# Empty space between x and the weights, four reorderings, in a two-model forward pass on one core

## The chip, the cores and the metric

The kernel runs on one core of a Trainium2 chip. The metric is device time in microseconds. Before the change the median of three runs is 2032.73 us (2032.72 to 2033.11). The one execution that the profiler recorded took 2020.3 us, of which its span, from the first to the last instruction, is 2018.6 us.

## The reference

One sequence of 256 tokens, width 1024, float32, goes through two models, one after the other.

- The first: a norm, `h @ w_in`, a gated linear recurrence over heads of 64 (`S_t = diag(f_t) S_{t-1} + k_t v_t^T`, `o_t = S_t^T q_t`), a short causal convolution, a gated merge and `w_out`; then a layer of 16,384 single-neuron experts. A query `h @ w_query` is scored against two sets of 128 keys per head, the best 16 of each set make 256 candidates, the best 16 of these are kept, and `out = sum gate * gelu(u_i . h) * v_i` over them.
- The second: two layers, each `x + 0.5 * swiglu(norm(x))`, a mixer (stick-breaking attention with pooling in the even layer, block attention in the odd one), and again `x + 0.5 * swiglu(norm(x))` with 2816 hidden units.
- A norm stands at the end of each.

## The kernel before, in words

Every activation is held transposed, 128 channels by 256 tokens. `x`, `xh` and `xl` are tiles of 8 x 256 float32 for the residual and the two halves of the normed input. Every weight matrix is cut into blocks of 128 x 128, 5220 in all, and eight blocks in the order of use are a chunk, one transfer of 512 KB.

A product at nearly full float32 precision takes three matmuls in the type float32r (`mm3`, lines 149 to 154): the weights' high half times the input's high half, the weights' high half times the input's low half, the weights' low half times the input's high half. The weights are the stationary operand, 128 x 128; the input is the moving one, 128 x 256. For this ScalarE rounds a raw chunk into `whi` (line 80) and VectorE subtracts to get `wlo` (line 87). There are five buffers for `raw`, four for `whi`, three for `wlo`, each 4096 bytes in a partition.

`boundary(c)` (line 91) runs when the program comes to a new chunk. It queues the splits and loads of the chunks ahead, then functions that were hooked to a chunk number (`hook`, line 124), then one step of each running generator (`side`, line 127). So the order of each engine's queue is the order of the Python code. All loads go through SyncE's queue.

Places that the change touches:

- **Start** (lines 412 to 454). `x` comes in pieces of two rows and the first three chunks in halves, by turns; `vec` (all gains and small vectors, 108 columns) and `ident` go through ScalarE's queue. Then pairs of rows are scaled into `xh` and `xl` and the half chunks are split.
- **Recurrence** (`hgrn`, line 677). The generator `decays` (line 695) makes cumulative decays at six block lengths. At each: two Exp on ScalarE (lines 713, 714), an addition into `su` (line 717) that may only overwrite `su` when the second Exp has read it, then a `yield`, then an addition into `pr` (line 720), which the next length's Exp reads. The main generator multiplies the results into `qk` (lines 763, 764) and TensorE makes scores of them (line 742).
- **Rank table** (line 863). Three chunks into the query stage a hook loads all keys, 1 MB; one chunk later another loads `iota`, and VectorE at once makes `ranks` from it.
- **ffn** (line 487). 22 blocks of 128 hidden units: gate and up products from `xh`, `xl`; the activation is split into `ah`, `al` (tiles of 1024 bytes); then the down products, eight blocks of weights for each `ah`. The four calls are a0, b0, a1, b1.
- **Last norm** (`final`, line 369). Six small matmuls sum the squares, POOL and VectorE make `1/sqrt`, TensorE spreads it over the partitions, VectorE copies it to `R`, and `x` is multiplied by it in four pieces (VectorE three, POOL one of two rows) that are stored as they come.

Where the operands lie follows from the order and sizes of the tiles. In the built program `xh` and `xl` begin at bytes 9,344 and 17,536 of each partition, the weights' buffers at 53,056 and every 4,096 on. Taken modulo 512 that is 128 for the inputs and 320 for the weights. A block is 512 bytes and a row of the input 1024, so the distance from the weights to the moving operand, modulo 512, is the same for every block: 320 for `xh`, `xl`; 0 for `ah`, `al` in all four ffn stages and for `oh`, `ol` in the odd mixer; 384 for `oh`, `ol`, `mph`, `mpl` in the even mixer; 160 for `mh`, `ml`, `yah`, `ybh` of the first mixer.

Of the kernel before, what the change touches and what calls it, by code (L numbers as in the profile page):

```python
# [10 lines left out]
F32 = mybir.dt.float32  # L11
# [21 lines left out]
STAGES = 3  # L33
RANK = 256
PACE = 1.0
FF = 22
NBLOCKS = 5220
NCHUNK = -(-NBLOCKS // CB)
# [11 lines left out]
class Net:  # L50
# [318 lines left out]
    def final(self):  # L369
        nc = self.nc  # L370
        V, S, G, mm = nc.vector, nc.scalar, nc.gpsimd, nc.tensor.matmul
        ps = self.sm.tile([P, 512], F32, name="sm")
        parts = [self.ssum] + self.last
        for t in range(2):
            for j, q in enumerate(parts):
                mm(ps[:, t:t + 1], q[:, t * P:(t + 1) * P], self.ones, start=(t == 0 and j == 0),
                   stop=(j == len(parts) - 1), skip_group_check=True)
        r = self.rsqrt_b(*self.rsqrt_a(ps[:, 0:2], 2, 1.0 / D))
        ps = self.sm.tile([P, 2, T], F32, name="sm")
        self.bcast(ps[:, 0, :], r)  # L380
        R = self.sqp.tile([P, T], F32, name="R", bufs=1)
        V.tensor_copy(R, ps[:, 0, :])
        for i in range(4):
            s = slice(2 * i, 2 * i + 2)
            if i < 3:
                V.tensor_tensor(self.x[:, s, :], self.x[:, s, :],
                                R[:, None, :].to_broadcast([P, 2, T]), op=ALU.mult)
            else:
                for k in (6, 7):
                    G.tensor_tensor(self.x[:, k, :], self.x[:, k, :], R, op=ALU.mult)  # L390
            o = self.out[2 * i * P:(2 * i + 2) * P, :].rearrange("(k p) t -> p k t", p=P)
            (nc.sync if i < 3 else nc.scalar).dma_start(o, self.x[:, s, :])

    def out_tail(self, name, ks, sl, first, alpha, gcol):
        for i in range(KD // 2):
# [6 lines left out]
    def run(self, first=0, last=99):  # L402
        nc, tc = self.nc, self.tc
        pool = tc.tile_pool
        with pool(name="base", bufs=1) as base, pool(name="sqp", bufs=2) as self.sqp, \
                pool(name="small", bufs=2) as self.small, \
                pool(name="rawp", bufs=self.NRAW) as self.rawp, \
                pool(name="hip", bufs=self.NHI) as self.hip, \
                pool(name="lop", bufs=self.NLO) as self.lop, \
                pool(name="accp", bufs=4, space=PSUM) as self.acc, \  # L410
                pool(name="smp", bufs=4, space=PSUM) as self.sm:
            A = self.A
            self.x = base.tile([P, KD, T], F32, name="x")
            self.xh = base.tile([P, KD, T], F32R, name="xh")
            self.xl = base.tile([P, KD, T], F32R, name="xl")
            self.vec = base.tile([P, NV], F32, name="vec")
            self.ident = base.tile([P, P], F32, name="ident")
            self.ones = base.tile([P, 1], F32, name="ones")
            self.mhalf = base.tile([P, 16], F32, name="mhalf")
            nc.scalar.dma_start(self.vec, A["vec"])  # L420
            nc.scalar.preload_act_table_set("natural_log_exp_and_others")
            hw = CB * P // 2
            for i in range(self.NRAW):
                if i > 2:
                    self.load_chunk(i)
                    continue
                self.raws[i] = self.rawp.tile([P, CB * P], F32, name="raw")
                for j in range(2):
                    if i < 2:
                        k = slice(4 * i + 2 * j, 4 * i + 2 * j + 2)  # L430
                        nc.sync.dma_start(self.x[:, k, :], A["x"][:, k, :])
                    h = slice(j * hw, j * hw + hw)
                    nc.sync.dma_start(self.raws[i][:, h], A["w"][i][:, h])
            nc.scalar.dma_start(self.ident, A["ident"])
# [6 lines left out]
            for i in range(self.NHI):  # L441
                if i > 2:
                    self.split_hi(i)
                    continue
                self.his[i] = self.hip.tile([P, CB * P], F32R, name="whi")
                self.los[i] = self.lop.tile([P, CB * P], F32R, name="wlo")
                for j in range(2):
                    if i < 2:
                        for k in (4 * i + 2 * j, 4 * i + 2 * j + 1):
                            self.norm_k(k, self.gain(GAINS[first]))  # L450
                    h = slice(j * hw, j * hw + hw)
                    nc.scalar.copy(self.his[i][:, h], self.raws[i][:, h])  # L452
                    nc.vector.tensor_tensor(self.los[i][:, h], self.raws[i][:, h], self.his[i][:, h],
                                            op=ALU.subtract)
# [13 lines left out]
            for i, st in enumerate(stages):  # L468
                if i > last:
                    break  # L470
                if i < first:
                    continue
                nxt = None if i == len(stages) - 1 else self.gain(GAINS[i + 1])
                st(nxt)
            if last < 90:
                for _ in self.norm_steps():
                    pass
                self.drain_sides()
                for k in range(KD):
# [7 lines left out]
    def ffn(self, tag, gcol):  # L487
        nc = self.nc
        with self.tc.tile_pool(name="ffn" + tag, bufs=3) as wp, \
                self.tc.tile_pool(name="ffa" + tag, bufs=8) as ap:  # L490
            ah = {}

            def ev(f, ps):
                gu = wp.tile([P, 2, T], F32, name="gu")
# [40 lines left out]
    def mixer1(self, gcol):  # L535
        nc = self.nc
        V, S = nc.vector, nc.scalar
        with self.tc.tile_pool(name="m1", bufs=1) as p1, self.tc.tile_pool(name="m1t", bufs=2) as tp:
# [17 lines left out]
            for z in (u[:, :, 0:2], su, ends[:, :, 1], sa, sb):  # L556
                nc.gpsimd.memset(z, 0.0)

            def vt(n):
                return tp.tile([P, 2, T], F32, name=n)  # L560
# [116 lines left out]
    def hgrn(self, ph, qp, E, pr, su, sa, sb, kk, qq, v, masks, oT, hg, late, outs):  # L677
# [7 lines left out]
        def half(t, c, which):  # L685
            return flat(t).rearrange("p (n two c) -> p n two c", two=2, c=c)[:, :, which, :]
# [8 lines left out]
        def decays():  # L695
# [15 lines left out]
            for li, c in enumerate(levels):  # L711
                up, low, nb = half(pr, c, 1), half(pr, c, 0), cols // (2 * c)
                S.activation(half(E[:, li], c, 1), up, AF.Exp)
                S.activation(half(E[:, li], c, 0), half(su, c, 0), AF.Exp)
                if li == nl - 1:
                    return
                V.tensor_tensor(half(su, c, 0), half(su, c, 0),
                                up[:, :, c - 1:c].to_broadcast([P, nb, c]), op=ALU.add)
                yield
                V.tensor_tensor(up, up, low[:, :, c - 1:c].to_broadcast([P, nb, c]), op=ALU.add)  # L720
        self.side(decays())
        yield
# [117 lines left out]
    def peer(self, gcol):  # L840
        nc = self.nc
        V, S, mm = nc.vector, nc.scalar, nc.tensor.matmul
        with self.tc.tile_pool(name="pe", bufs=1) as p1, self.tc.tile_pool(name="peh", bufs=2) as hp:
# [14 lines left out]
            live = top[0]  # L858
            kr, qr, xr = rows(8), rows(6), rows(8)
            keys = flat[:, kr * T:(kr + 8) * T].rearrange("p (h s n) -> p h s n", h=PH, s=2)  # L860
            self.hook(self.c + 3, lambda: nc.sync.dma_start(keys, self.A["keys"]))

            def consts():
                nc.sync.dma_start(self.iota, self.A["iota"])
                V.tensor_scalar(self.ranks, self.iota[:, 0:TOPK], float(RANK), None, op0=ALU.mult)
            self.hook(self.c + 4, consts)
            qv = [acts[:, qr + 2 * i:qr + 2 * i + 2, :] for i in range(3)]
            xn = acts[:, xr:xr + 8, :]

# [562 lines left out]
```

## Time and profile before

| | |
|---|---|
| median of three runs | 2032.73 us |
| the profiled execution, its own time | 2020.3 us |
| its span | 2018.6 us |
| TensorE busy | 1984.7 us, 98% |
| VectorE, ScalarE, POOL busy | 66%, 53%, 8% |
| mean granted clock of TensorE | 0.994 |
| data moved | 349.5 MB, 173 GB/s |

TensorE is the engine to look at. Its matmuls overlap, each shown for some 0.28 us though the next starts after about 0.118 us, so that its busy share says only where it stood still, not how fast it went; the pace is read from starts, or from how many matmuls fall into a window.

### The profile page before, as it was taken

The page shows a single profiled execution, that of the slowest core. Times are in us where ns is not written, and L with a number is a line of the kernel's source. Part 1 is how long each engine was busy: PE and PEld are TensorE (multiplying, and loading weights), DVE is VectorE, ACT ScalarE, POOL GpSimd, SP SyncE. Part 2 cuts the span into 40 slices and gives each one's busy share as a digit, 9 for nine tenths or more (in the row PEclk, how much of TensorE's full clock was granted, in tenths as well). Part 3 has the DMA queues.
Part 4 walks back from the last instruction along what each step waited for, and adds up shares of the span by engine and source line. Part 5 has one row for each costly group of instructions (what it writes and reads, how often), then busy time and mean ns, then how long its engine had stood idle before and what let it go on. Part 6 is the DMA issues. An engine that isn't in the chain of part 4 may idle for free.

```text
span 2018.6 us, 40539 instructions
## 1 busy us (share of the span) xinstructions
PE 1984.7 (98%) x16678; PEld 1956.7 (97%) x16678; DVE 1340.0 (66%) x2122; ACT 1072.6 (53%) x1754; POOL 170.2 (8%) x159
## 2 busy tenths in 40 slices
PE   8899899999999999999999999999999999999998
PEld 8899899999999999999999999999999999899997
DVE  6867578877777655555567556665566556666555
ACT  6454444557776545445464445654455445555444
POOL 2000244100000000000000001110001001231001
PEclk9999999999999999999999999999999999999999
DMA  7335445544444566666555555455555555435553
GB/s 243 128 130 182 164 168 189 188 167 141 143 139 134 164 194 196 193 195 197 191 167 193 184 188 192 146 172 185 187 180 187 188 186 179 160 129 188 185 184 103
DMA packets 97465, 349.50 MB, mean 173 GB/s; under 512 B 10880, under 2 KB 12416, under 8 KB 97152
## 3 DMA queue, kind: packets, MB, share of 16 engines
q1 hardware_dynamic: 96720, 346.53, 51.8%
q8 instruction: 130, 2.13, 0.4%
q10 hardware_dynamic: 560, 0.38, 0.1%
q14 instruction: 55, 0.45, 0.1%
HBM read 345.82 MB, written 1.05 MB: 172 GB/s over the span
## 4 chain that ended last, share of the span: by engine, by line
PE 96%; DVE 2%; DMA 1%; ACT 1%; issue 0%; POOL 0%; DVEq 0%; SPq 0%; ACTq 0%
PE acc L152 22%; PE acc L153 21%; PE acc L154 21%; PE sm L152 8%; PE sm L154 8%; PE sm L153 7%; PE sm L1127 3%; PE acc L176 1%; PE acc L177 1%; PE acc L178 1%; DVE wlo L87 1%; PE sm L742 0%; DMA iota<-in_iota 0%; PE sm L889 0%; POOL rs L251 0%
## 5 line engine op out<-in xcount | busy, mean ns | idle before, releaser
L87 DVE TENSOR_TENSOR wlo<-raw,whi 128x1024 fp32r<-128x1024 f32 x629 | 769.9, 1226 | 437.8 <-issue 241.7
L80 ACT CAST whi<-raw 128x1024 fp32r<-128x1024 f32 x650 | 679.2, 1049 | 499.1 <-PE acc L153 288.3
L152 PE MATMUL acc<-xh,whi 128*128 128x256 f32 x2848 | 804.9, 283 | 8.1 <-ACT whi L452 7.2
L154 PE MATMUL acc<-xh,wlo 128*128 128x256 f32 x2848 | 794.5, 279 | 3.7 <-DVE wlo L87 3.7
L153 PE MATMUL acc<-xl,whi 128*128 128x256 f32 x2848 | 794.5, 279 | 0.3
L152 PEld LDWEIGHTS acc<-xh,whi 128*128 128x128 f32 x2848 | 537.1, 189 | 13.2 <-ACT whi L452 7.2
L154 PEld LDWEIGHTS acc<-xh,wlo 128*128 128x128 f32 x2848 | 536.7, 188 | 4.7 <-DVE wlo L87 4.5
L153 PEld LDWEIGHTS acc<-xl,whi 128*128 128x128 f32 x2848 | 536.9, 189 | 0.9 <-DVE xl L220 0.7
L152 PE MATMUL sm<-xh,whi 128*128 128x256 f32 x1280 | 359.1, 281 | 0.0
L153 PE MATMUL sm<-xl,whi 128*128 128x256 f32 x1280 | 357.2, 279 | 0.0
L154 PE MATMUL sm<-xh,wlo 128*128 128x256 f32 x1280 | 357.1, 279 | 0.0
L152 PEld LDWEIGHTS sm<-xh,whi 128*128 128x128 f32 x1280 | 240.6, 188 | 0.0
L154 PEld LDWEIGHTS sm<-xh,wlo 128*128 128x128 f32 x1280 | 240.5, 188 | 0.0
L153 PEld LDWEIGHTS sm<-xl,whi 128*128 128x128 f32 x1280 | 239.9, 187 | 0.0
L154 PE MATMUL acc<-ah,wlo 128*128 128x256 f32 x704 | 199.5, 283 | 0.0
L152 PE MATMUL acc<-ah,whi 128*128 128x256 f32 x704 | 199.3, 283 | 0.0
L153 PE MATMUL acc<-al,whi 128*128 128x256 f32 x704 | 199.2, 283 | 0.0
L152 PEld LDWEIGHTS acc<-ah,whi 128*128 128x128 f32 x704 | 134.9, 192 | 0.0
L154 PEld LDWEIGHTS acc<-ah,wlo 128*128 128x128 f32 x704 | 134.6, 191 | 0.0
L153 PEld LDWEIGHTS acc<-al,whi 128*128 128x128 f32 x704 | 134.6, 191 | 0.0
L239 POOL TENSOR_TENSOR ssum<-ssum,sq 128x256 f32<-128x256 f32 x54 | 61.0, 1130 | 797.4 <-issue 575.6
L497 ACT ACTIVATE s<-gu 128x256 f32<-128x256 f32 x88 | 36.7, 418 | 119.8 <-DVE gu L314 119.5
(318 smaller groups left out, 1942.9 us busy)
## 6 DMA issues: line engine op xcount, KB each, us to landing
raw<-in_w SPq DMA_DIRECT2D x650, 512.0 KB, 3.7
raw<-in_w SPq DMA_DIRECT2D x6, 256.0 KB, 5.6
x<-in_x SPq DMA_DIRECT2D x4, 256.0 KB, 5.0
acts<-in_keys SPq DMA_DIRECT2D x1, 1024.0 KB, 7.7
out_dram<-x SPq DMA_DIRECT2D x3, 256.0 KB, 2.2
inv<-in_inv SPq DMA_DIRECT2D x1, 512.0 KB, 6.1
E<-in_masks SPq DMA_DIRECT2D x1, 320.0 KB, 7.9
out_dram<-x ACTq DMA_DIRECT2D x1, 256.0 KB, 2.4
```

The lines of the kernel that those rows point to most:

```text
L80: self.nc.scalar.copy(self.his[i], self.raws[i])
L87: e.tensor_tensor(self.los[i], self.raws[i], self.his[i], op=ALU.subtract)
L152: mm(out, wh, xh, start=start, stop=False, skip_group_check=True)
L153: mm(out, wh, xl, start=False, stop=False, skip_group_check=True)
L154: mm(out, wl, xh, start=False, stop=stop, skip_group_check=True)
L176: mm(pss[t], xh, wh, start=(k == 0), stop=False)
L177: mm(pss[t], xh, wl, start=False, stop=False)
L178: mm(pss[t], xl, wh, start=False, stop=(k == KD - 1))
L239: nc.gpsimd.tensor_tensor(self.ssum, self.ssum, sq, op=ALU.add)
L497: nc.scalar.activation(s, gu[:, 0, :], AF.Silu)
L1127: nc.tensor.matmul(ps[:, q, :], a[:, q, :], b[:, q, :], start=True, stop=True, skip_group_check=True)
```

## The change

Five edits, of which the first is one of place and the others are of order.

- **Empty space.** An unused tile of 128 bytes now lies between `xl` and all that follows, the weights' buffers among it. Another lies ahead of `ah` in each ffn stage: 64, 128, 256 and 384 bytes in a0, b0, a1, b1. The distance modulo 512 from the weights to the moving operand becomes 192 for `xh`, `xl` (from 320) and 64, 128, 256 and 384 for `ah`, `al` (from 0). The other tiles move along with the weights and keep theirs.
- **Rank table.** The keys come in eight pieces, one a chunk, `iota` with the first, and `ranks` is made 12 chunks later than before.
- **Recurrence.** The `yield` in `decays` stands ahead of the addition into `su` rather than behind it.
- **First loads.** The first gain alone, then the first chunk in quarters through ScalarE's queue, `x` in single rows through SyncE's; the rest later. VectorE instead of POOL clears `sa`.
- **Last norm.** The sums go part by part; VectorE and ScalarE read the spread factor from two PSUM tiles, VectorE without a copy; POOL multiplies one row and VectorE seven.

```diff
+SKEW = {"x": 128, "a0": 64, "b0": 128, "a1": 256, "b1": 384}
...
-        for t in range(2):
-            for j, q in enumerate(parts):
+        for j, q in enumerate(parts):
+            for t in range(2):
...
-        V.tensor_copy(R, ps[:, 0, :])
...
+        S.copy(R, ps[1][:, 0, :])
+        G.tensor_tensor(self.x[:, 7, :], self.x[:, 7, :], R, op=ALU.mult)
+        rows = lambda a, b: self.out[a * P:b * P, :].rearrange("(k p) t -> p k t", p=P)
+        for a, b, q in ((0, 2, nc.sync), (2, 4, nc.sync), (4, 6, nc.sync), (6, 7, nc.sync), (7, 8, nc.scalar)):
+            if b < 8:
+                V.tensor_tensor(self.x[:, a:b, :], self.x[:, a:b, :],
+                                ps[0][:, 0:1, :].to_broadcast([P, b - a, T]), op=ALU.mult)
+            q.dma_start(rows(a, b), self.x[:, a:b, :])
...
             self.xl = base.tile([P, KD, T], F32R, name="xl")
+            base.tile([P, SKEW["x"] // 4], F32, name="skew")
...
+            nc.scalar.dma_start(self.vec[:, g0:g0 + KD], A["vec"][:, g0:g0 + KD])
...
+            for k in range(4):
+                nc.scalar.dma_start(self.raws[0][:, two[k]], A["w"][0][:, two[k]])
+                nc.sync.dma_start(self.x[:, k, :], A["x"][:, k, :])
...
             ah = {}
+            ap.tile([P, SKEW[tag] // 4], F32, name="skew", bufs=1)
...
+                yield
                 V.tensor_tensor(half(su, c, 0), half(su, c, 0),
                                 up[:, :, c - 1:c].to_broadcast([P, nb, c]), op=ALU.add)
-                yield
...
-            self.hook(self.c + 3, lambda: nc.sync.dma_start(keys, self.A["keys"]))
-
-            def consts():
-                nc.sync.dma_start(self.iota, self.A["iota"])
-                V.tensor_scalar(self.ranks, self.iota[:, 0:TOPK], float(RANK), None, op0=ALU.mult)
-            self.hook(self.c + 4, consts)
+            for h in range(PH):
+                self.hook(self.c + 2 + h, lambda h=h: nc.sync.dma_start(keys[:, h], self.A["keys"][:, h]))
+
+            self.hook(self.c + 2, lambda: nc.sync.dma_start(self.iota, self.A["iota"]))
+            self.hook(self.c + 16, lambda: V.tensor_scalar(self.ranks, self.iota[:, 0:TOPK], float(RANK), None,
+                                                           op0=ALU.mult))
```

The order of TensorE's matmuls stays as it was, but for the six small ones of the last norm. Two places on VectorE move.

VectorE's queue in the recurrence before, from the first block length on; `su` and `pr` are the running sums, `t` and `u` belong to the convolution:

```order
L751 TENSOR_TENSOR qk<-E,kk 128x1024
L717 TENSOR_TENSOR su<-su,pr 128x128x4
L314 TENSOR_TENSOR t<-acc,R 128x512
L587 TENSOR_TENSOR u<-t 128x256
L87 TENSOR_TENSOR wlo<-raw,whi 128x1024
L720 TENSOR_TENSOR pr<-pr 128x128x4
L717 TENSOR_TENSOR su<-su,pr 128x64x8
L87 TENSOR_TENSOR wlo<-raw,whi 128x1024
```

The same place now, with the new line numbers (729 is the addition into `su`, 731 that into `pr`, 89 the split):

```order
L762 TENSOR_TENSOR qk<-E,kk 128x1024
L316 TENSOR_TENSOR t<-acc,R 128x512
L598 TENSOR_TENSOR u<-t 128x256
L89 TENSOR_TENSOR wlo<-raw,whi 128x1024
L729 TENSOR_TENSOR su<-su,pr 128x128x4
L731 TENSOR_TENSOR pr<-pr 128x128x4
L89 TENSOR_TENSOR wlo<-raw,whi 128x1024
L729 TENSOR_TENSOR su<-su,pr 128x64x8
```

Each addition into `su` moved behind the next chunk's split, next to the addition into `pr`.

VectorE's queue at the start of the query before; `rs` are the small tiles of the norm's `1/sqrt`:

```order
L87 TENSOR_TENSOR wlo<-raw,whi 128x1024 x4
L865 TENSOR_SCALAR ranks<-iota 128x16
L246 TENSOR_SCALAR rs<-sm 128x2
L87 TENSOR_TENSOR wlo<-raw,whi 128x1024
L256 TENSOR_TENSOR rs<-rs 128x2
```

And now:

```order
L89 TENSOR_TENSOR wlo<-raw,whi 128x1024 x4
L248 TENSOR_SCALAR rs<-sm 128x2
L89 TENSOR_TENSOR wlo<-raw,whi 128x1024
L258 TENSOR_TENSOR rs<-rs 128x2
L259 TENSOR_TENSOR rs<-rs 128x2
```

`ranks` left this place; it now stands 48 rows further on, amid the search for the best keys.

## Rows read from the trace of the kernel before

**Rows 1.** The page: busy time, share of the span, instructions of each engine.

```profile
PE 1984.7 (98%) x16678; PEld 1956.7 (97%) x16678; DVE 1340.0 (66%) x2122; ACT 1072.6 (53%) x1754; POOL 170.2 (8%) x159
```

**Rows 2.** Waits of TensorE, whole span: us in total, times, longest.

```profile
PE sm L291 <- DVE rs L259: 9.3, 2, 7.4
PE acc L152 <- ACT whi L452: 7.2, 1, 7.2
PE sm L742 <- DVE qk L764: 4.4, 1, 4.4
```

**Rows 3.** Groups by line, TensorE: names, shapes xcount | busy us, mean ns | idle before.

```profile
L152 PE MATMUL acc<-xh,whi 128*128 128x256 f32 x2848 | 804.9, 283 | 8.1 <-ACT whi L452 7.2 <-ACT xh L219 0.9
...
L152 PE MATMUL sm<-xh,whi 128*128 128x256 f32 x1280 | 359.1, 281 | 0.0
...
L152 PE MATMUL acc<-ah,whi 128*128 128x256 f32 x704 | 199.3, 283 | 0.0
```

**Rows 4.** Windows: PE, PEld, DVE, ACT, POOL busy (instructions), clock, DMA share, GB/s.

```profile
300.00:400.00 100.00, 100.00 (x852) 100.00 (x851) 88.15 (x307) 48.65 (x57) 29.15 (x12) 1.00 0.55 187
720.00:1020.00 300.00, 300.00 (x2650) 300.00 (x2649) 172.15 (x221) 149.41 (x220) 0.00 (x0) 1.00 0.60 194
```

**Rows 5.** Timeline of TensorE, first and last of a pass: start us, us, instruction.

```profile
190.13 0.28 PE L154 MATMUL acc<-mh,wlo 128*128 128x256 f32 x1
...
212.31 0.28 PE L154 MATMUL acc<-mh,wlo 128*128 128x256 f32 x1
...
1226.33 0.29 PE L152 MATMUL acc<-ah,whi 128*128 128x256 f32 x1
...
1240.38 0.28 PE L152 MATMUL acc<-ah,whi 128*128 128x256 f32 x1
...
1314.71 0.28 PE L154 MATMUL acc<-oh,wlo 128*128 128x256 f32 x1
...
1325.75 0.28 PE L154 MATMUL acc<-oh,wlo 128*128 128x256 f32 x1
```

**Rows 6.** Waits of TensorE from 60 to 90 us (the recurrence).

```profile
PE acc L154 <- DVE wlo L87: 2.6, 2, 1.9
```

**Rows 7.** Waits of VectorE from 60 to 82 us.

```profile
DVE su L717 <- ACT E L714: 4.9, 4, 1.2
```

**Rows 8.** Windows with the clock at half, columns as in rows 4.

```profile
82.70:87.60 4.90, 4.89 (x30) 4.78 (x31) 4.49 (x6) 3.04 (x4) 0.00 (x0) 0.50 0.59 203
235.10:237.80 2.70, 2.70 (x14) 2.70 (x13) 2.67 (x5) 0.00 (x0) 0.00 (x0) 0.50 0.66 228
```

**Rows 9.** Waits of VectorE from 210 to 250 us (start of the query).

```profile
DVE ranks L865 <- DMA iota<-in_iota: 8.5, 1, 8.5
```

**Rows 10.** Timeline of SyncE's queue there: start, us, issues.

```profile
222.81 0.38 SPq L861 DMA_DIRECT2D acts<-in_keys  x1
...
223.90 1.05 SPq L864 DMA_DIRECT2D iota<-in_iota  x1
```

**Rows 11.** Timeline of ScalarE from 0 us: first work after the loads.

```profile
5.68 0.91 ACT L219 ACTIVATE xh<-x,vec 128x256 fp32r<-128x256 f32 x2 [3.17 <-DMA vec<-in_vec]
6.50 0.60 ACT L452 CAST whi<-raw 128x512 fp32r<-128x512 f32 x1
```

**Rows 12.** Timeline of TensorE from 0 us.

```profile
7.15 0.58 PE L152 MATMUL acc<-xh,whi 128*128 128x256 f32 x1 [7.15 <-ACT whi L452]
```

**Rows 13.** Timeline of TensorE at the end.

```profile
2007.98 0.38 PE L376 MATMUL sm<-ones,R 128*128 128x1 f32 x2
...
2008.67 0.36 PE L376 MATMUL sm<-ones,R 128*128 128x1 f32 x2
```

**Rows 14.** Timeline of VectorE at the end.

```profile
2011.72 0.42 DVE L382 COPY R<-sm 128x256 f32<-128x256 f32 x1 [0.92 <-PE sm L291]
2012.18 2.95 DVE L386 TENSOR_TENSOR x<-x,R 128x512 f32<-128x512 f32 x3
```

**Rows 15.** Timeline of VectorE: a product that reads PSUM.

```profile
59.90 0.68 DVE L314 TENSOR_TENSOR t<-acc,R 128x512 f32<-128x512 f32 x1
```

More of the change, by code (lines that the diff above doesn't have):

```diff
@@ L378, in final @@
         r = self.rsqrt_b(*self.rsqrt_a(ps[:, 0:2], 2, 1.0 / D))
-        ps = self.sm.tile([P, 2, T], F32, name="sm")
-        self.bcast(ps[:, 0, :], r)
+        ps = [self.sm.tile([P, 2, T], F32, name="sm") for _ in range(2)]
+        for p in ps:
+            self.bcast(p[:, 0, :], r)
         R = self.sqp.tile([P, T], F32, name="R", bufs=1)
-        V.tensor_copy(R, ps[:, 0, :])
[L383 to L392, printed above, removed]
+        S.copy(R, ps[1][:, 0, :])
[6 more added lines that the diff above has]
+            q.dma_start(rows(a, b), self.x[:, a:b, :])
     def out_tail(self, name, ks, sl, first, alpha, gcol):
@@ L419, in run @@
             self.mhalf = base.tile([P, 16], F32, name="mhalf")
[L420 to L434 removed]
+            g0 = VCOLS[GAINS[first]]
+            rest = [c for c in ((0, g0), (g0 + KD, NV)) if c[0] < c[1]]
+            nc.scalar.dma_start(self.vec[:, g0:g0 + KD], A["vec"][:, g0:g0 + KD])
+            for i in range(3):
+                self.raws[i] = self.rawp.tile([P, CB * P], F32, name="raw")
+            hw = CB * P // 2
+            two = [slice(k * 2 * P, (k + 1) * 2 * P) for k in range(4)]
+            halves = [slice(0, hw), slice(hw, 2 * hw)]
+            for k in range(4):
+                nc.scalar.dma_start(self.raws[0][:, two[k]], A["w"][0][:, two[k]])
+                nc.sync.dma_start(self.x[:, k, :], A["x"][:, k, :])
+            nc.scalar.preload_act_table_set("natural_log_exp_and_others")
+            for j in range(2):
+                nc.sync.dma_start(self.x[:, 4 + 2 * j:6 + 2 * j, :], A["x"][:, 4 + 2 * j:6 + 2 * j, :])
+                nc.sync.dma_start(self.raws[1][:, halves[j]], A["w"][1][:, halves[j]])
+            for h in halves:
+                nc.sync.dma_start(self.raws[2][:, h], A["w"][2][:, h])
+            for u, v in rest:
+                nc.sync.dma_start(self.vec[:, u:v], A["vec"][:, u:v])
+            self.load_chunk(3)
+            nc.sync.dma_start(self.ident, A["ident"])
+            self.load_chunk(4)
             nc.vector.memset(self.ones, 1.0)
@@ L440, in run, with begin @@
             nc.vector.memset(self.hsel[64:128, 1:2], 1.0)
[L441 to L449, printed above, removed]
-                            self.norm_k(k, self.gain(GAINS[first]))
[L451 to L454, printed above, removed]
+            def begin():
+                for i in range(3):
+                    self.his[i] = self.hip.tile([P, CB * P], F32R, name="whi")
+                    self.los[i] = self.lop.tile([P, CB * P], F32R, name="wlo")
+                    for j, h in enumerate(two if i == 0 else halves):
+                        for k in ([j], [4 + 2 * j, 5 + 2 * j], [])[i]:
+                            self.norm_k(k, self.gain(GAINS[first]))
+                        nc.scalar.copy(self.his[i][:, h], self.raws[i][:, h])
+                        nc.vector.tensor_tensor(self.los[i][:, h], self.raws[i][:, h], self.his[i][:, h],
+                                                op=ALU.subtract)
+                self.split_hi(3)
+            self.begin = begin
             self.norm_pending, self.first_c = True, 1
@@ L555, in mixer1 @@
             ends = E[:, len(LEVELS) + 3].rearrange("p a t -> p (a t)").rearrange("p (n c) -> p n c", c=BASE)
-            for z in (u[:, :, 0:2], su, ends[:, :, 1], sa, sb):
+            nc.vector.memset(sa, 0.0)
+            for z in (su, sb, ends[:, :, 1], u[:, :, 0:2]):
                 nc.gpsimd.memset(z, 0.0)
+            self.begin()
             def vt(n):
```

## The prediction

> **What bounds the kernel now.** I read the page's busy line first, then TensorE's waits, then its pace. TensorE is busy 98% of the span [rows 1], so only two things can move the time: the stretches where it stands still, and how fast matmul follows matmul while it does not. The other engines matter where they make TensorE wait.
>
> Of the waits the reader is to see how few they are [rows 2]: 9.3 us for `rs` of the norms, 7.2 us for the first weights, 4.4 us for the first `qk` of the recurrence; 2.6 us more for `wlo`, in the recurrence too [rows 6]. Together that is about 24 us, 1.2% of the span.
>
> The pace is larger. Nearly everything is one shape, 128x128 times 128x256, and the mean duration, 281 to 283 ns, hides the pace since the instructions overlap [rows 3]. Count instead. From 300 to 400 us (the expert layer's U) 852 instructions touch the window; some 2.4 of them began before it (0.28 us each at this pace), so 100 us / 849.6 = 117.7 ns apiece. From 720 to 1020 us (V), 300 us / 2647.5 = 113.3 ns [rows 4]. Same shape, same full clock, same operands `xh` and `xl` at the same distance (320) from the weights: 4% apart. So at this distance there are two paces, and what decides which is not in the code's order.
>
> Other distances can be read from passes of eight output blocks [rows 5], counting the starts of one of the three lines: at 160 (`mh`, 64 blocks, 189 steps in 22.18 us) 117.35 ns; at 384 (`oh` of the even mixer, 32 blocks, 93 steps in 11.04 us) 118.7 ns; at 0 (`ah`, 40 blocks, 117 steps in 14.05 us) 120.1 ns. The clock is full in all of them, so the place of the moving operand is the likely cause, and 0 is the slowest place seen.
>
> **The change, part by part.** The sum is made against the profiled execution's 2020.3 us (span 2018.6 and 1.7 around it). That lies 12.4 us under the median, 2032.7. The fast stretch of V may be all of it: some 3,070 matmuls (348 us at 113.3 ns) at 117.7 would take 13.5 us more. I take it that the timed runs had no such stretch; that is an inference.
>
> *Rank table.* VectorE waits 8.5 us for `iota` [rows 9], issued behind 1 MB of keys [rows 10]; behind that wait in its queue stand the norm's small steps, and TensorE waits 7.4 us for them [rows 2]. On its return the clock is at half: 14 matmuls in 2.70 us [rows 8], 1.65 us at full pace, so 1.05 us more. The change takes `ranks` from this place and I see nothing else late: without the wait VectorE would run the norm's steps some 8 us sooner. The keys still land well before the scores that need them, one head a chunk. Gain 8.5; 7 at least if another wait of 1.5 us remains, 8.5 at most.
>
> *Recurrence.* The addition into `su` waits for ScalarE's second Exp four times, 4.9 us [rows 7], while VectorE is late for TensorE: 2.6 us for `wlo` [rows 6] and 4.4 us for `qk` [rows 2]. Moved one chunk on, it finds the Exp done. The next length's Exp starts one addition later, 0.7 us, which ScalarE's idle time covers; were it not covered, six lengths would cost 4 us. I take the 4.9 us off TensorE's 7.0, 2.1 remain. After the 4.4 us the clock was at half for 4.90 us [rows 8], worth 2.4 us; the `wlo` waits of 1.9 us and less brought no such stretch, so I count it as gone. Gain 7.3; from 1 to 9.4.
>
> *First loads.* Before, the first matmul waits for two rows of `xh` (0.91 us) and a half chunk (0.60 us) after the loads land at 5.68 [rows 11], and starts at 7.15 [rows 12]. One row and a quarter come to roughly 0.45 + 0.42. Gain 0.6, if the smaller loads land when the larger did; from a loss of 1.5 (they share ScalarE's queue and are more in number) to a gain of 1.5. Clearing `sa` on VectorE is hidden, since VectorE has nothing to do until the loads land.
>
> *Last norm.* Three small matmuls fewer behind the last square, 2008.67 - 2007.98 = 0.7 us [rows 13]; no copy of `R`, 0.45 us; the products end 2.95 us after they begin [rows 14] and would take 3 x 0.68 [rows 15] + 0.42 = 2.5 us from PSUM. Gain 1.6; from 0.5 to 2.3.
>
> These four: 8.5 + 7.3 + 0.6 + 1.6 = 18.0 us.
>
> *Place of `ah`, `al`.* 3 x 704 = 2112 matmuls [rows 3], 528 a stage, now at 120.1. The new distances: 64 lies between 0 and 160 and I take 119.0 by a straight line; 128 likewise 117.9; 256 between 160 and 320, 117.5; 384 is measured, 118.7. Gain 528 x (1.1 + 2.2 + 2.6 + 1.4) ns = 3.9 us. Ends: all at 113.3 gains 14.4; as far above 120.1 as that lies above 117.7 loses 5.1.
>
> *Place of `xh`, `xl`.* 3 x (2848 + 1280) = 12,384 matmuls [rows 3], so each nanosecond is 12.4 us, and the new distance, 192, is in no row. The nearest is 160: 117.35 ns. By it the 3,070 fast ones lose 4.05 ns (12.4 us) and the other 9,314 gain 0.35 (3.3 us): 9.1 us more than in the profiled execution, but 4.3 us less than in runs that were at 117.7 throughout. Ends: 113.3 and 120.1 for all of them.
>
> Sum: 2020.3 - 18.0 - 3.9 + 9.1 = 2007.5. From the median: 2032.7 - 18.0 - 3.9 - 4.3 = 2006.5. The two agree because both put V at the same pace. I predict 2007 us.
>
> *A rule that speaks against the second half.* The trace shows three paces at three distances at full clock [rows 4, 5]. The Trainium skill's page "SBUF — State Buffer", section "SBUF: two separate sides", says that TensorE's reads never wait for anyone, and that contention is confined to a port pair of VectorE and GpSimd; by it empty space could change nothing. The trace does not agree in one respect: with the same shape and clock, 113.3 to 120.1 ns are seen, though no row separates place from everything else in those passes.
>
> **The rivals.**
>
> *Place does nothing.* The differences come from what each stage does beside the matmuls (V and U also differ in how they visit PSUM), and `xh` stays at its pace. For it: U and V differ by 4% at one distance. Against it: `ah` sits at 120 in a stage where `xh`, between the same splits, sits near U's pace. Then only the four reorderings count: 2032.7 - 18.0 = 2014.7.
>
> *The low pace is held.* At 192 the matmuls fall into 113.3 ns and stay. For it: V stays there for 300 us without a break. Against it: all long stretches at 320 but this one ran at 117.7. 12,384 x 4.4 ns = 54.5 us: 2032.7 - 21.9 - 54.5 = 1956.
>
> *The new place is as bad as 0.* Mechanism: the moving operand's and the weights' reads meet at 192 in every matmul as they seem to at 0, and all 12,384 run at 120.1. Price 12,384 x 2.4 = 29.7 us: 2032.7 - 21.9 + 29.7 = 2040.5, slower. It decides from 21.9 us / 12,384 = 1.8 ns above 117.7, that is from 119.5 ns. For it: one distance of the four measured is that bad, and nothing says what 192 is. Against it: 160 and 320, on both sides, are not.
>
> *The stalls come back.* VectorE sets the pace around the recurrence; if its `qk` is late all the same and the clock falls again, and the first loads land later, half of the 18 us is lost: 2032.7 - 9 - 3.9 = 2020 with `xh` unmoved.
>
> **How the numbers follow.** Forecast (117 to 118.5 ns at 192, stalls gone; its own range 1999 to 2021) 0.36; low pace held, wholly or for most stages (1956 to 1990) 0.25; place does nothing 0.14; as bad as 0 (2028 to 2041) 0.15; stalls come back 0.10. A measurement of this kernel tells about 0.2%, 4 us, from no change: under 2028.7 is faster, over 2036.8 slower. All of the forecast, the low pace and "does nothing" are faster, and half of the stalls' case: 0.36 + 0.25 + 0.14 + 0.05 = 0.80. Of the bad place 0.12 is slower; its rest and the rest of the stalls' case is the same, 0.08. The range goes from the low pace held, 1956, to 2032, leaving out the worse part of the bad place and a pace below any row.
>
> **What would show it.** The rank table: no wait for `iota` on VectorE and no half clock near 235 us. The recurrence: no wait of the `su` addition on ScalarE, a wait for `qk` near 2 us, full clock after it. The end: last store about 1.6 us nearer to the last sum. Place: instructions in 100 us of gate and up, of U, and in 300 us of V; and the passes of `ah`, which must differ between a0, b0, a1 and b1 if place counts and be alike at 120 if it does not. The prediction is wrong if the matmuls at 192 run under 116.5 ns or over 119 ns, or if TensorE still stands for over 4 us near 80 or 230 us.

## The result, and the profile after

The changed kernel takes 1984.37 us, the median of five runs (1979.02 to 1987.89). The kernel before, run beside it, took 2032.72. The ratio is 0.977, with a 95% interval of 0.975 to 0.980. The forecast was 2007 us; the time lies in its range (1956 to 2032), 23 us under its point, and in the case that stood there as a rival, "the low pace is held" (1956 to 1990).

Single runs of the kernel before fall into two groups, 13 of 41 between 2016.5 and 2021.5 us and 28 between 2029.5 and 2034.3, and the execution whose profile the prediction was made from belongs to the first.

The profiled execution after took 1984.37 us, its span is 1982.6. The page's busy line (busy us, share of the span, instructions):

```profile
PE 1961.3 (99%) x16680; PEld 1934.3 (98%) x16680; DVE 1342.6 (68%) x2125; ACT 1073.3 (54%) x1757; POOL 167.0 (8%) x157
```

TensorE is busy for 23 us less than before [rows 1], with the same matmuls but for two more small ones in the last norm. So most of the gain is not waits that went. Its waits over the whole span (us in total, times, longest):

```profile
PE acc L154 <- ACT whi L458: 6.6, 1, 6.6
PE sm L753 <- DVE qk L775: 3.0, 1, 3.0
PE sm L293 <- DVE rs L261: 1.9, 1, 1.9
PE acc L156 <- DVE wlo L89: 1.5, 2, 1.2
```

Against [rows 2, 6]: the norm's `rs` went from 9.3 us to 1.9, which is the last norm alone; `qk` from 4.4 to 3.0; the 1.5 us for `wlo` stand elsewhere, since from 60 to 90 us only the 3.0 for `qk` are left. In all TensorE stands still for 21.3 us (1982.6 - 1961.3) where it stood 33.9: 12.6 of the 36.0 us by which the span got shorter. The timeline has the first matmul 0.6 us sooner than [rows 12]:

```profile
6.55 0.58 PE L154 MATMUL acc<-xh,whi 128*128 128x256 f32 x1 [6.55 <-ACT whi L458]
```

The stretches that had a half clock (columns: window, us busy and instructions of TensorE, granted clock, DMA share, GB/s):

```profile
75.80:82.90 7.10, 7.10 (x41) 0.52 0.57 199
219.00:238.00 19.00, 19.00 (x167) 1.00 0.63 222
```

The stretch near 235 us [rows 8] is gone. The one behind the `qk` wait is not. It looks longer than the 4.9 us of [rows 8], but it isn't: there the clock had already fallen while TensorE still waited. The first line is of the kernel before, ahead of the window in [rows 8]; the second is of the changed kernel:

```profile
80.80:82.70 1.90, 0.00 (x0) 0.50 0.14 43
76.10:82.90 6.80, 6.80 (x40) 0.50 0.57 198
```

Half the clock was granted for 6.8 us both times, from 80.8 to 87.6 us and from 76.1 to 82.9. Before, 1.9 us of it fell into the wait; now all of it falls on matmuls.

Now the pace. Windows of the kernel before in the four ffn stages a0, b0, a1, b1 (same columns):

```profile
1100.00:1200.00 100.00, 100.00 (x845) 1.00 0.56 185
1380.00:1480.00 100.00, 100.00 (x845) 1.00 0.56 186
1560.00:1660.00 100.00, 100.00 (x846) 1.00 0.56 186
1850.00:1945.00 95.00, 95.00 (x803) 1.00 0.55 184
```

And of the changed kernel, in U, in V and with the same borders in the four stages, which hold these windows in both:

```profile
300.00:390.00 90.00, 90.00 (x766) 1.00 0.57 187
720.00:1020.00 300.00, 300.00 (x2650) 1.00 0.61 195
1100.00:1200.00 100.00, 100.00 (x873) 1.00 0.57 191
1380.00:1480.00 100.00, 100.00 (x860) 1.00 0.59 188
1560.00:1660.00 100.00, 100.00 (x868) 1.00 0.58 189
1850.00:1945.00 95.00, 95.00 (x815) 1.00 0.58 189
```

U and V run as in [rows 4], one at the slow pace (766 instructions in 90 us, 117.8 ns by their starts) and one at the fast (2650 in 300 us, 113.3), although the weights have moved by 128 bytes against `xh`. The ffn stages got faster by 1.5 to 3.3%. Split by pass, from the starts in the timeline: gate and up took 117.85 ns in all four stages before, from the first down product on; after, 113.5 in a0, 113.7 in a1, and in b0 and b1 passes at 117.8 and 113.9 by turns. The down products of `ah` took 120.1 in all four; after, 117.8 at distance 64, 118.7 at 128, 119.2 at 256 and 118.7 at 384.

### The profile page after: what moved, and what is told of

Same layout as the page of the kernel before. It is cut to its first block, busy times and chain, and to the rows that moved or that the text cites. A ratio compares the mean times of both kernels' runs of the same rounds, so it can differ in the third digit from the quotient of the medians.

```text
span 1982.6 us, 40567 instructions
## 1 busy us (share of the span) xinstructions
PE 1961.3 (99%) x16680; PEld 1934.3 (98%) x16680; DVE 1342.6 (68%) x2125; ACT 1073.3 (54%) x1757; POOL 167.0 (8%) x157
## 4 chain that ended last, share of the span: by engine, by line
PE 96%; DVE 2%; ACT 1%; issue 0%; POOL 0%; DMA 0%; DVEq 0%; ACTq 0%; POOLq 0%
PE acc L154 22%; PE acc L156 21%; PE acc L155 21%; PE sm L154 8%; PE sm L155 8%; PE sm L156 7%; PE sm L1138 3%; PE acc L179 1%; PE acc L178 1%; PE acc L180 1%; DVE wlo L89 1%; PE sm L753 0%; PE sm L900 0%; PE sm L1345 0%; PE sm L1320 0%
## 5 line engine op out<-in xcount | busy, mean ns | idle before, releaser
L154 PEld LDWEIGHTS acc<-xh,whi 128*128 128x128 f32 x2848 | 537.7, 189 | 12.6 <-ACT whi L458 6.6
```

What stands on the lines that cost most here:

```text
L154: mm(out, wh, xh, start=start, stop=False, skip_group_check=True)
```

## The experiments

Two theories stood at the start: place (each pace follows the distance from the weights to the moving operand), and its rival, that order and waits did it all.

### The halves of the change

`order_only` is the changed kernel without the empty space; `space_only` is the kernel before with the empty space.

```diff
-            base.tile([P, SKEW["x"] // 4], F32, name="skew")
...
-            ap.tile([P, SKEW[tag] // 4], F32, name="skew", bufs=1)
```

> The four reorderings with no empty space: distances 320 for xh and 0 for ah as before. If place decides which of the two paces a pass takes, the gate and up passes stay at 117.8 ns and the ah passes at 120.1 in all four ffn stages, and only the stalls go: the stretch from the start to the long run of U is some 15 us shorter, the ffn stages are as long as before (about 164 us from first to last ah), and the time is near 2032.7 - 16 = 2017, or 13 less where V falls into 113.3 ns. If place does nothing and the reorderings changed the phase at which the stages are entered, the ffn stages are 3 to 5 us shorter each as in the changed kernel, and the time is near 1984.

> The empty space alone, in the old order. If place decides: ffn a0 has gate and up at 113.5 and ah at 117.8; b0 and b1 have gate and up by turns at 113.5 and 117.8 and ah at 118.8; a1 has 113.5 and 119.2; the four stages are together 16 us shorter than before, all stalls are as before, and the time is near 2032.7 - 20 = 2013, or 13 less with a fast V. If the reorderings did it, the ffn passes are at 117.8 and 120.1 and the time is near 2032.7.

Measured: `order_only` 2015.26 us (ten runs, 2001.71 to 2018.85), ratio to before 0.992 (0.990 to 0.995). `space_only` 1993.82 (1991.65 to 1997.11), ratio 0.985 (0.980 to 0.990). Both halves count. `space_only` came out 6 us under the lower of the two times that were expected for it; its profile shows the reason. Two of its windows, U and a0, then those of `order_only`, with the borders of above:

```profile
300.00:390.00 90.00, 90.00 (x797) 1.00 0.60 198
1100.00:1200.00 100.00, 100.00 (x873) 1.00 0.58 191
```

```profile
300.00:390.00 90.00, 90.00 (x766) 1.00 0.57 188
720.00:1020.00 300.00, 300.00 (x2549) 1.00 0.57 187
1100.00:1200.00 100.00, 100.00 (x845) 1.00 0.55 185
1380.00:1480.00 100.00, 100.00 (x846) 1.00 0.56 185
1560.00:1660.00 100.00, 100.00 (x845) 1.00 0.56 185
1850.00:1945.00 95.00, 95.00 (x803) 1.00 0.56 185
```

In `space_only` the ffn is that of the changed kernel, in all four windows to within one instruction, and U too runs at the fast pace (797 in 90 us, 113.3 ns), worth 5.4 us against the changed kernel, which has the same distance there. In `order_only` the ffn is that of before, to within one instruction. And V, with 2549 in its window, runs at 117.8 ns, so that this execution took 2018.51 us though it has the reorderings. V's pace changes from run to run with nothing changed in the program: the stretch with V takes 388.8 us in the profile of before and 402.0 here, and the 13.2 us between them are about the gap between the two groups of the kernel before. That the group of 2030 has V at the slow pace is inferred, not seen: no profile of before fell into it.

Where the reorderings gained is read from the starts of passes, before and in `order_only`: up to a pass of the recurrence that started at 90.0 and now 85.9, counted from 44.3 and 44.5, 4.3 us; from the end of the `mh` pass (212.4; 208.3) to the long run of U (277.4; 264.4), 8.9; from the last down product to the end (11.8; 10.8), 1.0. The first matmul starts at 7.17, no earlier than before.

`rank_only` is the kernel before with the edit of the rank table alone (the hooks on chunks 2 to 9 and 16 of the diff).

> The kernel before with the rank table's edit alone. My reading of the trace: no wait of VectorE for iota, the last chunk of the query's first pair starts 7.4 us sooner and at full clock, from the end of the mh pass to the start of the long U run 8.5 us less (56.5 instead of 65.0), everything ahead of it as before: 2024.2 (or 2011.8 if V takes its faster pace). Rival: another wait takes the place of the one for iota (the keys' last pieces, or the norm's small steps), and 4 us or less is gained there.

Measured: 2022.2 us, one run, with V at 117.8 ns in its profile. From the `mh` pass to U 56.1 us (210.4 to 266.5) where there were 65.0: 8.9. The clock there (all engines, then clock, DMA share, GB/s):

```profile
212.00:240.00 28.00, 28.00 (x239) 27.75 (x238) 18.91 (x37) 13.57 (x19) 9.54 (x9) 1.00 0.61 207
```

TensorE has no pause and no half clock in this stretch; what the wait for `iota` did, it did alone.

### Other distances

`x_at_0` puts `xh` and `xl` at distance 0; `ladder2` puts them at 256 and `ah` at 192, 320, 448 and 32.

```diff
-SKEW = {"x": 128, "a0": 64, "b0": 128, "a1": 256, "b1": 384}
+SKEW = {"x": 320, "a0": 64, "b0": 128, "a1": 256, "b1": 384}
```

```diff
-SKEW = {"x": 128, "a0": 64, "b0": 128, "a1": 256, "b1": 384}
+SKEW = {"x": 64, "a0": 192, "b0": 320, "a1": 448, "b1": 32}
```

> The changed kernel with 320 bytes instead of 128 behind xl, so that xh and the weights are 0 apart modulo 512; the distances of ah are kept (64, 128, 256, 384). If the distance sets the pace, all products of xh (U, V, gate and up) run at 120 ns, as ah did at 0 before: 12,384 matmuls, of which some 7,500 were at 113.4 and 4,900 at 117.8, lose 7,500 x 6.6 + 4,900 x 2.2 = 60 us, time near 2045. If place does nothing, U stays at 117.8, V at 113.3 and the time is near 1984.

> The changed kernel with other distances: xh at 256 (64 bytes behind xl), ah at 192, 320, 448 and 32 in a0, b0, a1 and b1. If the pace depends on the distance alone and on its size, not its sign, a0 and b0 (192 and -192) have the same ah pace, 113.3 or 117.8; a1 (-64) has 117.8 as a0 of the changed kernel had at 64; b1 (32) lies between that and 120.1. xh at 256 I don't know: between 113.3 and 119.8, the values seen for ah at 256 and for xh at 192. If place does nothing, all four ffn stages look alike.

Measured, one run each: 2035.85 us (near 2045 was expected, had place set the pace) and 2029.62 us. First `x_at_0`, then `ladder2`:

```profile
300.00:390.00 90.00, 90.00 (x752) 1.00 0.55 186
720.00:1020.00 300.00, 300.00 (x2503) 1.00 0.55 183
```

```profile
300.00:390.00 90.00, 90.00 (x753) 1.00 0.57 186
720.00:1020.00 300.00, 300.00 (x2502) 1.00 0.55 183
1100.00:1200.00 100.00, 100.00 (x851) 1.00 0.56 186
```

2502 and 2503 in 300 us are 120.0 ns. U takes the same, gate and up 119.6 to 120.1. So place does set the pace, and 256 is as bad as 0: distances count modulo 256, not 512 as the prediction had them. Then `ah` should run alike at 192 and 448, which it does in `ladder2`: 114.2 ns at both (118.0 at 320 and at 32). A pace by the size of the distance whatever its sign, as the expectation weighed it, would have made 192 and 320 alike. The old place of `xh`, 320, is 64 in this count.

### Which of the two spaces matters

`x_space` keeps only the space behind `x`; `ah_space` only those in the ffn.

> The changed kernel without the empty space in the ffn pools: xh stays at distance 192 from the weights, the ffn activations ah lie at distance 0 as before. Theory A (each product's pace follows its own distance): ah at 120.1 ns in all four ffns, gate and up at 113.5 to 117.8 as xh at 192 allows; time 1984.4 plus 528 ah products per ffn times 2.3, 1.4, 0.7 and 1.4 ns, 3.1 us: 1987.5 if gate and up keep their paces. Theory B (which of two paces gate and up take is set by the pass entered just before them, the ah pass): with ah at 120.1 gate and up fall back to 117.85 in all four ffns, 816 products times 4.3 ns in a0 and a1 and half of it in b0 and b1, 10 us more: about 1997.

> The changed kernel without the empty space behind x: xh at distance 320 as before, ah at 64, 128, 256 and 384. Theory A: ah at 117.8, 118.7, 119.2 and 118.7 ns, gate and up at 117.9 in all four ffns (as before at 320): 2015.3 (the reordered kernel without space) less 3.1 us, 2012, or about 2000 if the V products take the faster of their two paces. Theory B: gate and up at 113.5 in a0 and a1 and alternating in b0 and b1, as in the changed kernel: 10 us less, 2002 (1990 with V at the faster pace).

Measured, one run each: 1983.04 and 2000.47 us. The second is what theory A has with V at the faster pace; the first lies under both theories. Windows of `x_space`, then of `ah_space`:

```profile
1100.00:1200.00 100.00, 100.00 (x868) 1.00 0.58 190
1380.00:1480.00 100.00, 100.00 (x868) 1.00 0.58 188
```

```profile
720.00:1020.00 300.00, 300.00 (x2650) 1.00 0.61 195
1100.00:1200.00 100.00, 100.00 (x851) 1.00 0.56 186
1380.00:1480.00 100.00, 100.00 (x849) 1.00 0.57 186
```

With `xh` at 192 and `ah` at 0, gate and up run at 113.7 ns in all four stages, better by the mean than in the changed kernel, and `ah` itself at 119.2. That in b0 and b1 they got faster with the spaces of `ah` gone is more than A can say and the opposite of B. With `xh` at 320 gate and up stay at 117.8, wherever `ah` lies. So the space behind `x` does the work. With it in place the spaces of `ah` do none: from the start of the first down product to that of the last the four stages take 161.2 us each without them, 160.1, 162.5, 161.2 and 162.5 with them, 1.6 us more in all. Without it they do a little, as theory A has it: 163.8, 164.3, 165.1 and 164.3 us in `ah_space` against 165.1 each in `order_only`, 3.0 us less.

### What decides between the two paces

`all192` puts everything of the ffn at 192; `ladder3` and `ladder4` put `ah` at other distances.

```diff
-SKEW = {"x": 128, "a0": 64, "b0": 128, "a1": 256, "b1": 384}
+SKEW = {"x": 128, "a0": 192, "b0": 192, "a1": 192, "b1": 192}
```

> The changed kernel with ah at distance 192 in all four ffns (it ran at 114.1 ns there, and at 113.5 in the tail, in the run with the second set of distances). Theory A: ah 3.7, 4.6, 5.1 and 4.6 ns below the changed kernel's, times 528 products each, 9.5 us; gate and up at 113.5 in b0 and b1 too, 1.6 us each: about 1972 (1966 to 1977). Theory B (a pace that two operands at one place share falls to the slower of the two): gate, up and ah all near 117.8: about 1991. Rival C, the pace is no matter of the distance: 1984.

Measured: 1981.48 us (1978.45 to 1985.22), about the changed kernel's. None of the three theories had this:

```profile
1100.00:1200.00 100.00, 100.00 (x851) 1.00 0.56 187
1380.00:1480.00 100.00, 100.00 (x852) 1.00 0.58 185
1560.00:1660.00 100.00, 100.00 (x885) 1.00 0.59 193
1850.00:1945.00 95.00, 95.00 (x809) 1.00 0.56 187
```

Stage a1 runs at 113.3 ns in every pass, `xh` and `ah` alike (885 in 100 us); the other three at 117.8 in every pass. Same code, same places. At this distance TensorE keeps, for a whole stage, the pace with which it came in: in the gate and up pass ahead of the first down product it ran at 113.7 ns in a1 and at 117.8 in the other three. It is not the pace of the stage before: V ended at 113.3 ns and a0 began at 117.8, b0 ended at 117.8 and a1 began at 113.7, each with the small matmuls of a norm between them.

> The changed kernel with ah at distances 96, 224, 160 and 16 in the four ffns, xh at 192. Theory A with straight lines between the distances measured so far (64: 117.8, 128: 118.7, 160: 117.3, 192: 113.5, 256 and 0: 120.0, 32: 117.8): ah at 118.2, 117, 117.3 and 119 ns; about 1983. A theory in which only multiples of 32 and not the distance itself matter would give 117.8 in the first three and 120 at 16.

> The changed kernel with ah at distances 176, 208, 240 and 48 in the four ffns. If the pace varies smoothly between the distances measured so far: 115.0, 116, 119.5 and 117.8 ns; by theory D gate and up at 113.4 to 114.0 in all four, since each down pass at another place leaves the faster pace behind it; the four ffns take 158.8, 159.3, 161.5 and 160.5 us from first to last ah, about 1972 or 1978 with the long U run at 113.3 or at 117.8. If instead only 192 has a fast pace: all four ah at 117.3 to 120.

Measured, one run each: 1972.4 and 1981.77 us. `ladder3`: gate and up at 113.7 to 114.0 in all four stages; `ah` at 119.4 (96), 118.1 (224), 117.3 (160) and 116.7 ns. The straight lines between distances fail. Space is rounded up to 32 bytes, as the built program shows, so the 16 was 32, and `ladder4` measured 192, 224, 256 and 64 rather than what its expectation names: 117.8, 118.1, 119.2 and 117.9 ns, with gate and up at 117.8, 114.0, 113.7 and 117.7. It says nothing on smoothness, and its stage at 64 differs from a0 of the changed kernel, at 64 too, where gate and up ran at 113.5. The two were entered at different paces: ahead of the first down product gate and up ran at 117.8 ns in the one and at 113.4 in the other. So a pass at 64 seems to leave the running pace as it is.

Theory D came from the runs up to `ladder3`: at 192 the running pace goes on, and a pass at 0, 32, 96, 160 or 224 leaves the fast one behind it. `kick` tests it: `ah` at 448, which counts as 192, but the first tile of each stage at 256.

```diff
-SKEW = {"x": 128, "a0": 64, "b0": 128, "a1": 256, "b1": 384}
+SKEW = {"x": 128, "a0": 256, "b0": 256, "a1": 256, "b1": 256}
...
+            first = [ap.tile([P, T], F32R, name="f" + n, bufs=1) for n in ("ah", "al")]
+            ap.tile([P, 48], F32, name="skew2", bufs=1)
...
-                hi, lo = ap.tile([P, T], F32R, name="ah"), ap.tile([P, T], F32R, name="al")
+                hi, lo = first if f == 0 else (ap.tile([P, T], F32R, name="ah"), ap.tile([P, T], F32R, name="al"))
```

> The kernel with all at distance 192, but the first activation tile of each ffn alone (24 of its down products) at distance 256. Theory D (at 192 there are two paces, 113.3 and 117.8, and the one that runs goes on until a pass at another distance is entered, which leaves the faster one behind it): from the first down products on gate, up and ah all at 113.3 in all four ffns, each 157.8 to 158.5 us from first to last ah, against 160.2 to 162.9 in the changed kernel; 12 us less than its 1984.4, about 1972 (1966 where the long U run takes 113.3 too). Rival E (the pace is drawn at random at the start of each stretch, whatever ran before): the ffns mix 157.8 and 164.0 as in the run with all at 192; 1978 to 1985.

Measured: 1966.66 us (1962.6 to 1977.53), ratio to before 0.967 (0.965 to 0.969).

```profile
720.00:1020.00 300.00, 300.00 (x2550) 1.00 0.56 187
1100.00:1200.00 100.00, 100.00 (x885) 1.00 0.55 191
1380.00:1480.00 100.00, 100.00 (x884) 1.00 0.56 191
1560.00:1660.00 100.00, 100.00 (x884) 1.00 0.58 194
1850.00:1945.00 95.00, 95.00 (x841) 1.00 0.59 194
```

All four stages run at 113.3 ns and take 157.8 us each, from the start of the first down product to that of the last. The change can be seen where it happens. Here are windows of b0 ahead of those 24 down products and behind them, gate and up in both:

```profile
1325.00:1330.00 5.00, 5.00 (x45) 1.00 0.42 145
1334.40:1339.40 5.00, 5.00 (x47) 1.00 0.72 257
```

By their starts that is 117.8 ns, then 113.8 for the first pass and 113.3 from there on. Three of the four stages were entered at the slow pace and left it there; a0 was entered at the fast one and kept it. Rival E is out for the ffn. V was at 117.8 in this execution (2550), which is the slowest of the five, 1977.53.

`kick_uv` does the same for the expert layer: row 1 of U's input and the second moving tile of V lie at 0, which counts as 256.

```diff
+            z = [p1.tile([P, T], F32R, name="z" + n) for n in "hl"]
...
-                    self.mm3(ps[:, j % 2, :], "U", k, j, self.xh[:, k, :], self.xl[:, k, :],
+                    self.mm3(ps[:, j % 2, :], "U", k, j, *(z if k == 1 else (self.xh[:, k, :], self.xl[:, k, :])),
...
-                    ws[j] = (self.xh[:, j % 8, :], self.xl[:, j % 8, :])
+                    ws[j] = z if j == 1 else (self.xh[:, j % 8, :], self.xl[:, j % 8, :])
```

> The kernel with the first activation tile of each ffn at distance 256 and the rest at 192, and in the expert layer too one tile at distance 256: row 1 of the input of U (so 3 of each block's 24 matmuls run there) and the second moving tile of V (24 matmuls, once). Theory D (a pass at another distance leaves the faster pace at 192 behind it): U near 114.2 ns, 113.3 plus 6.7 in 3 of 24, also in the pieces between the selection's work, where 46 of 63 ran at 117.8; V at 113.3 from its 49th matmul to its end, in every run; the times of single runs then lie within 5 us of each other, at 1959 to 1965, where the kernel without this gave 1962.6 to 1977.5. Rival E (chance at each entry): V at 117.7 in about a third of the runs, and the times spread over 15 us as before.

Measured: 1962.35 us, its four runs from 1961.24 to 1964.2, as theory D has it. Its ratio to the runs of before beside it is 0.969 (0.965 to 0.974).

```profile
300.00:390.00 90.00, 90.00 (x790) 1.00 0.57 193
720.00:1020.00 300.00, 300.00 (x2650) 1.00 0.57 193
1100.00:1200.00 100.00, 100.00 (x885) 1.00 0.56 189
```

U is at 114.2 ns and V at 113.3; the ffn stages were all four entered at 117.8 ns and all four take 157.8 us, and the spread of single runs fell from 15 us to 3. This kernel is faster than both the one before and the changed one, 22 us under the latter by medians that were not taken side by side. For V it proves little. In the seven other kernels with `xh` at 192 the profiles have V slow in one; at that rate four fast runs come by chance in 0.54 (six sevenths to the fourth power), at a third, as the expectation had it, in 0.2. U is better placed: it was slow in three of those seven profiles, and of the some 63 short pieces of U between the selection's work 41 to 48 ran slow in each; here four did.

## Why the prediction was right in its sign and too high by 23 us

- **Place of `xh`: the step that failed.** The prediction gave all 12,384 matmuls the one pace of the nearest distance, 117.35 ns. The mean in the trace after is 115.05, and it is a mean over two paces: fast in gate and up for the most part and in V, slow in the long run of U. The difference is 2.30 ns times 12,384, 28.5 us, more than the whole error. By the prediction's own sign (matmuls at 192 under 116.5 ns) its account of place was wrong. That the time still lies in the range is owed to the low end, which stood there for a rival's sake. The profile had shown two paces at one distance [rows 4], and the prediction still asked what "the" pace at 192 is. The right question was what a place lets happen. At 320 no ffn stage ran fast after its first down products, in the 16 stages of four profiles; at 192 gate and up ran fast throughout in 23 of 32, by turns in four, and slow in five, where `ah` lay at 192 or 64. The rival "the low pace is held" had more of the mechanism (not all: it had every stage at 113.3, and U was not) and was held to be less likely, on the ground that the long stretches at 320 were mostly slow; that is no evidence on 192.
- **The median and the profiled run.** The inference that the runs at 2032 us had V slow, and so lay 12 us above the profile, is borne out as far as runs can: V took either pace in kernels whose order and places are the same up to there (`all192` and `kick`), and the runs of before form two groups of that distance. After the change V can still go either way, and so can U, slow in `all192` and fast in `kick`.
- **Place of `ah`.** Forecast 3.9 us off the down products by straight lines. Measured, their mean pace went from 120.07 to 118.71 ns: 2112 times 1.36, 2.9 us. But `x_space` shows that these spaces cost 1.6 us as a whole, for they take gate and up off the fast pace, by turns, at 128 and 384. Taking 256 for a place between 160 and 320 failed too: 117.5 ns was expected there, 119.2 measured. The term had the right size for the wrong quantity: what a pass does to the next one counts more than its own pace.
- **Rank table.** Forecast 8.5, measured 8.9 twice. Right, with the half clock behind the wait.
- **Recurrence.** Forecast 7.3, measured 4.3 in `order_only`. The stall of the `su` addition went, and TensorE's 7.0 us became 3.0 (forecast 2.1). But the half clock was counted as gone because a wait of 1.9 us had brought none. It came behind the wait of 3.0 us here and behind one of 2.2 us in `order_only`, for 6.8 us each, and in `ah_space`, with the same order and pace up to there, for 3.4 us, where the gain is 5.8. VectorE now has no idle time ahead of `qk`; `qk` is late by VectorE's own work. So a faster TensorE only waits longer for it: with the 144 matmuls ahead of this place at 119.9 ns (`x_at_0`), 117.8 (`order_only`) and 113.5 (the changed kernel) the wait is 1.8, 2.2 and 3.0 us, and behind the 1.8 us the clock stayed full. VectorE's queue up to `qk` in the changed kernel:

```profile
72.17 0.68 DVE L316 TENSOR_TENSOR t<-acc,R 128x512 f32<-128x512 f32 x1
72.89 0.43 DVE L598 TENSOR_TENSOR u<-t 128x256 f32<-128x256 f32 x1
73.23 1.22 DVE L89 TENSOR_TENSOR wlo<-raw,whi 128x1024 fp32r<-128x1024 f32 x1
74.37 0.69 DVE L774 TENSOR_TENSOR qk<-E,qq 128x512 f32<-128x512 f32 x1
74.97 0.69 DVE L775 TENSOR_TENSOR qk<-E,kk 128x512 f32<-128x512 f32 x1
```

- **First loads.** 0.6 forecast, and 7.15 became 6.55. But the first matmul starts anywhere from 6.01 to 7.17 us in the profiles of eleven kernels with this edit and from 6.76 to 7.15 in three without, so the term can't be told from chance by one profile.
- **Last norm.** Forecast 1.6, measured 1.0. The products took 2.21 us where they took 2.95 [rows 14], less than the 2.5 counted, but SyncE now issues four stores where it issued three, and its last issue ends 0.89 us behind the last product, before 0.43:

```profile
1976.39 2.21 DVE L390 TENSOR_TENSOR x<-x,sm 128x512 f32<-128x512 f32 x4 [0.92 <-PE sm L293]
...
1977.11 2.38 SPq L392 DMA_DIRECT2D out_dram<-x  x4
```

The account closes to about a microsecond: from the forecast's 2007.5, 28.5 off for `xh`, and 1.0, 3.0 and 0.6 on for `ah`, the recurrence and the last norm, 0.4 off for the rank table, make 1983.2; measured were 1984.37. It is no closer than that, since the recurrence and the first loads alone change by a microsecond or more from profile to profile.

The rule that was weighed, the Trainium skill's "SBUF — State Buffer", section "SBUF: two separate sides", by which TensorE's port never waits on anyone, does not hold up as a forecast of pace here: moving the weights against `xh` by nothing but empty space (the changed kernel and `x_at_0`) took V from 113.3 to 120.0 ns at full clock. Whether TensorE waits on itself there, its reads of weights against those of the moving operand, is not shown by any run; only the distance is.

## What to carry to other kernels

When one shape at one clock shows two paces, don't average or interpolate them: look at where each begins, and at what ran just before. In a kernel that TensorE bounds, measure the distance between stationary and moving operands as a size like any other, in whole stages and more than one run each, for a stage can keep to its end the pace with which it began. When a wait goes, look at the clock inside the wait as well as behind it. A large spread of single runs can be a pace drawn at entry, and then it can be taken away by design.

## What the runs showed of the hardware that was not expected

For float32r products of 128 x 128 by 128 x 256 at full clock, start to start, by the distance in bytes from the weights to the moving operand modulo 256:

| distance | ns, `xh` moving | ns, `ah` moving |
|---|---|---|
| 0 | 119.6 to 120.1 | 119.1 to 120.1 |
| 32 | | 116.7 and 118.0 |
| 64 | 117.8 or 113.3 | 117.8 to 118.0 |
| 96 | | 119.4 to 119.9 |
| 128 | | 118.6 to 118.9 |
| 160 | | 117.3 |
| 192 | 117.8 or 113.3 to 114.0 | 117.8, 114.2 or 113.3 |
| 224 | | 118.0 to 118.3 |

These are passes behind the first down product of a stage. At 192 a pace once taken was kept for over 150 us and through changes of tile and PSUM pool (`all192`); 24 matmuls at a distance that counts as 256 left the fast one behind them in all eight ffn stages of `kick` and `kick_uv`, seven of which had been entered at the slow one. At 64 such a pass does the opposite: in the kernel before, gate and up of a0, at 320, ran at 113.3 ns in the pass ahead of the first down pass at 0, and at 117.85 behind it and to the end of the stage. Why the two differ, what draws the pace where a stage begins, and what in the engine holds it, stays open.
